# Linear attentions: the score tiles of two heads in one tile of two banks, put together by the same instructions

## The chip, the cores and the metric

The kernel runs on 1 core of one Trainium2 chip. The metric is the device time of one execution in microseconds (us). Before the change it is 2995.86 us, the median of 3 runs (2993.44 to 3003.88). Engines are named as in the profile: PE (TensorE matmuls), PEld (its weight loads), DVE (VectorE), ACT (ScalarE), POOL (GpSimd), SP (the queue that issues the DMAs).

## The reference

One layer of a hybrid encoder on 2048 tokens of width 1024. A projection `p = RMSNorm(x) @ W_in` is split among four mixers: FoX attention, a gated delta net, HGRN2 and GLA, with 4 heads each; then an output projection and a feed-forward part. The change concerns the two linear attentions, HGRN2 (key width 64) and GLA (key width 32), both of this form:

```python
def gla_chunked(q, k, v, log_a, scale):
    ...
    G = jnp.cumsum(log_a..., axis=3)
    rel = jnp.where(causal[:, :, None], G[..., :, None, :] - G[..., None, :, :], -jnp.inf)
    a_intra = jnp.einsum('bhnrd,bhnsd,bhnrsd->bhnrs', q, k, jnp.exp(rel))
    o_intra = jnp.einsum('bhnrs,bhnse->bhnre', a_intra, v)
    ...
    def step(state, inp):
        o = jnp.einsum('bhcd,bhde->bhce', qi, state)
        state = state * ai[..., None] + jnp.einsum('bhcd,bhce->bhde', ki, vi)
```

The score of a row and an earlier column is a dot product weighted by a decay that differs for every key channel, so it is no plain product of two matrices.

## The kernel before, in words

**Streams.** The tokens go in 4 blocks of 512. `phase_mix` runs four streams and weaves them by due time: `group_gdn`, `group_hg` (HGRN2), `group_gla`, and `in_proj`, which makes the projections (`proj_fm`, `proj_tm`, `mm3` at lines 107 to 110: three 128x512 matmuls for each of 8 slices) and the operands of FoX. When the projections are done, FoX (`fox_stream`) is woven with what is left of the mixers. The framework then schedules the instructions of each engine by priority; what the projections need is given priority (`first`). The order on each engine is fixed when the program is built. Rows of the order below show it.

**One linear attention.** `group_hg` and `group_gla` call `lin_attn` with `nt` = 2 and 1 (the number of 128-row tiles that the 4 heads fill). It goes through a block in 4 chunks of 128 tokens. `operands` makes, for the 7 levels h = 64, 32, ..., 1, tiles `wx` in which queries and keys carry the decay from the middle of each stretch of 2h tokens (lines 690 to 709). With these a score between the two halves of such a stretch is a plain product.

**The products.** For one group `g`, line 726 takes a tile `ps2` of one PSUM bank (128 x 512 floats; the profile calls it `ps`) from a pool of two. A group covers two head-and-chunk pairs `u`: two heads of one chunk for HGRN2, one head in two chunks for GLA; in what follows it is called a head. For each `u`, line 732 makes the 32x32 products of levels 0, 1, 2, 4, 8 and 16 for four 32-token blocks, line 736 those of level 32 and line 739 those of level 64: 56 matmuls for a head, which the profile counts as 112.

**Putting together.** Line 742 (VectorE) multiplies level 0 by a diagonal mask into `l_acc`; line 744 overlays the five other levels with masked copies, 64 columns each. Lines 751 or 753 (ScalarE, four copies) bring the four diagonal blocks to `AT`, lines 756 and 758 (two copies each) the off-diagonal blocks straight from the score tile. `AT` is one fixed tile per attention. Line 770 then multiplies it with the values, beside line 767, which adds what the state gives; line 772 takes the result off, lines 776, 778 and 782 make the state's update, line 787 applies it.

So a block holds 8 groups of HGRN2 (4 chunks x 2) and 8 of GLA (2 pairs of chunks x 4), 64 in all for 4 blocks. Both attentions share the pool `ps2`; all others (`ps`, `psl`, and `ps_mm` of the projections) are their own pools.

## Time and profile before

| what | us |
|---|---|
| median of 3 runs | 2995.86 |
| the profiled execution | 2996.68 |
| its span, first to last instruction | 2994.9 |
| TensorE matmuls busy | 2864.3 |
| VectorE busy | 2152.0 |
| ScalarE busy | 1596.3 |
| mean granted TensorE clock (share of full speed) | 0.967 |

Times in the profile are from the first instruction. Busy time of matmuls is modelled at its end, so matmuls that follow each other closely overlap in it; the starts tell their pace. A wait is listed as the engine and line that waited, and the engine and line that came last. The profile drops buffer numbers, so `ps` stands for the tiles of the pools `ps` and `ps2` alike; lines tell them apart.

### The profile page before, as it was taken

What the parts mean: (1) busy time and instruction counts of PE and PEld (TensorE: products, weight loads), DVE (VectorE), ACT (ScalarE), POOL (GpSimd) and SP (SyncE); (2) the same over time, 40 slices, a digit from 0 to 9 for tenths busy, and PEclk for the clock granted to TensorE, in tenths of its full rate; (3) what the DMA queues carried; (4) which work ended last, traced back from release to release, by engine and by line L of the source; (5) the groups of instructions that cost most, each with busy time, mean ns of one, the idle gap of its engine ahead of it and who ended that gap; (6) DMA issues with size and microseconds to landing.
All of it is one profiled execution on the core that took longest, in us unless ns stands there. A gap on an engine that the chain in (4) does not pass through costs nothing.

```text
span 2994.9 us, 57398 instructions
## 1 busy us (share of the span) xinstructions
PE 2864.3 (96%) x21994; PEld 2335.9 (78%) x21994; DVE 2152.0 (72%) x4666; ACT 1596.3 (53%) x3171; POOL 127.5 (4%) x258
## 2 busy tenths in 40 slices
PE   7999999999999998999999999999999999999999
PEld 5777777787777777777788888878788888888787
DVE  6697778678767876667666655558777777886975
ACT  6575667566656665555666632343455544544443
POOL 0000010001000100000000000003000000000000
PEclk9999999799889997999999999999999999999999
DMA  5633463355235523876533322453222221847344
GB/s 179 183 100 126 139 181 100 112 165 166 80 104 171 165 66 103 222 205 203 137 107 103 102 67 66 141 184 116 85 84 75 85 85 60 281 142 242 130 136 145
DMA packets 268938, 400.08 MB, mean 134 GB/s; under 512 B 66612, under 2 KB 93124, under 8 KB 268152
## 3 DMA queue, kind: packets, MB, share of 16 engines
q1 hardware_dynamic: 268664, 396.43, 43.5%
q8 instruction: 172, 2.82, 0.4%
q14 instruction: 102, 0.84, 0.1%
HBM read 310.63 MB, written 85.70 MB: 132 GB/s over the span
## 4 chain that ended last, share of the span: by engine, by line
PE 73%; DVE 9%; DMA 9%; ACT 6%; issue 2%; SPq 0%; DVEq 0%; ACTq 0%
PE ps_mm L108 15%; PE ps_mm L109 15%; PE ps_mm L110 14%; PE pt L108 3%; PE pt L110 3%; PE pt L109 3%; DVE w_lo L307 2%; PE po L1033 2%; DMA w_raw<-w_fm 2%; PE pt L1019 2%; PE ps L732 1%; ACT w_hi L306 1%; PE ps_mm L344 1%; PE ps_mm L346 1%; PE ps_mm L347 1%
## 5 line engine op out<-in xcount | busy, mean ns | idle before, releaser
L307 DVE TENSOR_TENSOR w_lo<-w_raw,w_hi 128x512 fp32r<-128x512 f32 x386 | 268.8, 698 | 199.7 <-ACT w_hi L306 188.1
L306 ACT CAST w_hi<-w_raw 128x512 fp32r<-128x512 f32 x386 | 237.7, 617 | 281.2 <-PE ps_mm L109 179.4
L108 PE MATMUL ps_mm<-h_hi,w_hi 128*128 128x512 f32 x736 | 314.8, 429 | 15.7 <-ACT h_hi L300 7.7
L108 PE MATMUL ps_mm<-h,w_hi 128*128 128x512 f32 x768 | 308.2, 402 | 2.6 <-ACT h L1208 1.7
L109 PE MATMUL ps_mm<-h,w_hi 128*128 128x512 f32 x768 | 303.9, 396 | 0.0
L109 PE MATMUL ps_mm<-h_lo,w_hi 128*128 128x512 f32 x736 | 303.5, 413 | 0.0
L110 PE MATMUL ps_mm<-h,w_lo 128*128 128x512 f32 x768 | 303.4, 396 | 0.0
L110 PE MATMUL ps_mm<-h_hi,w_lo 128*128 128x512 f32 x736 | 302.1, 411 | 0.5 <-issue 0.4
L108 PE MATMUL ps_mm<-big,w_hi 128*128 128x512 f32 x456 | 183.6, 404 | 11.1 <-ACT big L306 6.7
L108 PEld LDWEIGHTS ps_mm<-h_hi,w_hi 128*128 128x128 f32 x736 | 144.3, 197 | 54.8 <-ACT h_hi L300 10.5
L110 PE MATMUL ps_mm<-big,w_lo 128*128 128x512 f32 x456 | 181.8, 399 | 0.0
L109 PE MATMUL ps_mm<-big,w_hi 128*128 128x512 f32 x456 | 181.7, 399 | 0.0
L110 PEld LDWEIGHTS ps_mm<-h,w_lo 128*128 128x128 f32 x768 | 144.4, 188 | 33.8
L108 PEld LDWEIGHTS ps_mm<-h,w_hi 128*128 128x128 f32 x768 | 144.1, 188 | 33.1 <-ACT h L1208 2.7
L110 PEld LDWEIGHTS ps_mm<-h_hi,w_lo 128*128 128x128 f32 x736 | 144.6, 196 | 31.0 <-DVE w_lo L307 1.5
L109 PEld LDWEIGHTS ps_mm<-h,w_hi 128*128 128x128 f32 x768 | 144.6, 188 | 30.9 <-DVE h L1209 1.4
L109 PEld LDWEIGHTS ps_mm<-h_lo,w_hi 128*128 128x128 f32 x736 | 144.6, 196 | 30.7 <-issue 3.2
L306 ACT CAST w_hi<-fo 128x512 fp32r<-128x512 f32 x135 | 79.5, 620 | 104.4 <-issue 36.8
L1238 DVE SCALAR_TENSOR_TENSOR y<-u,fconv,y 128x512 f32<-128x512 f32 x176 | 131.8, 749 | 3.8
L1382 DVE SCALAR_TENSOR_TENSOR y<-u,fconv,y 128x1024 f32<-128x1024 f32 x88 | 112.8, 1282 | 19.5 <-ACT y L1380 18.7
L307 DVE TENSOR_TENSOR p_lo<-pt,p_hi 128x512 fp32r<-128x512 f32 (+1 forms) x144 | 93.9, 657 | 37.9 <-ACT p_hi L306 37.8
L108 PE MATMUL pt<-w_hi 128*128 128x512 f32 x308 | 120.3, 391 | 0.0
(414 smaller groups left out, 7306.4 us busy)
## 6 DMA issues: line engine op xcount, KB each, us to landing
w_raw<-w_fm SPq DMA_DIRECT2D x184, 256.0 KB, 3.1
w_raw<-w_up SPq DMA_DIRECT2D x88, 256.0 KB, 2.6
fo<-w_down SPq DMA_DIRECT2D x88, 256.0 KB, 3.5
fo<-a_scr SPq DMA_DIRECT2D x88, 256.0 KB, 4.4
wr<-w_up SPq DMA_DIRECT2D x84, 256.0 KB, 2.7
p_scr<-w SPq DMA_DIRECT2D x72, 256.0 KB, 2.7
w_raw<-w_out SPq DMA_DIRECT2D x64, 256.0 KB, 3.7
w_raw<-w_tm SPq DMA_DIRECT2D x48, 256.0 KB, 3.0
```

What stands on the lines that cost most here:

```text
L108: mm(ps, w_hi, x_hi, start=start, stop=False, **k)
L109: mm(ps, w_hi, x_lo, start=False, stop=False, **k)
L110: mm(ps, w_lo, x_hi, start=False, stop=stop, **k)
L306: self.nc.scalar.copy(out=hi, in_=src)
L307: self.nc.vector.tensor_tensor(out=lo, in0=src, in1=f32(hi), op=ALU.subtract)
L344: mm(o, self.h_hi[k][:, ts], hi[:, s], start=(k == 0 and tt % 2 == 0), stop=False, skip_group_check=True)
L346: mm(o, self.h_hi[k][:, ts], lo[:, s], start=False, stop=False, skip_group_check=True)
L347: mm(o, self.h_lo[k][:, ts], hi[:, s], start=False, stop=(k == KT - 1), skip_group_check=True)
L1019: nc.tensor.transpose(pt[:, x * 128:x * 128 + 128], P[t][:, kt * 128:kt * 128 + 128], self.ident)
L1033: mm(po[:, c0:c0 + cn], vst[:, kt], part[:, kk * 256:kk * 256 + cn], start=(kt == 0 and part is hi), stop=(kt == nkt - 1 and part is lo), ...
L1238: nc.vector.scalar_tensor_tensor(out=y, in0=u[:, i:i + TB], scalar=w(i), in1=y, op0=ALU.mult, op1=ALU.add)
L1382: nc.vector.scalar_tensor_tensor(out=yt, in0=u[g][:, i:i + 2 * TB], scalar=f(i), in1=yt, op0=ALU.mult, op1=ALU.add)
```

## The change

The pool `ps2` holds one tile of two banks in place of two tiles of one bank. Two heads are multiplied into one such tile, one into each bank; then every instruction that puts a head together works on both: 4 copies from the score tile (lines 747 and 749, now ahead of VectorE's work), the multiplication (752), five masked copies (754) and four copies from `l_acc` (758). The generator yields once for two heads, with size 2.

```diff
@@ -172,7 +172,7 @@
             self.ch = pool(ctx, "ch", 2)
             self.ps = pool(ctx, "ps", 2, space=PSUM)
             self.psl = pool(ctx, "psl", 1, space=PSUM)
-            self.ps2 = pool(ctx, "ps2", 2, space=PSUM)
+            self.ps2 = pool(ctx, "ps2", 1, space=PSUM)
             cst = self.cst_p.tile([128, N_CST], F32, name="cst")
             nc.sync.dma_start(out=cst, in_=self.i["cst"])
             self.cst = cst
@@ -723,40 +723,40 @@
             if nt == 2 or c % 2 == 0:
                 ATg = self.AT[nt - 1]
                 ATs = [ATg[:, u] for u in range(3 - nt)]
-                for g in range(per):
-                    p = self.ps2.tile([128, TB], F32, name="ps2")
+                for g0 in range(0, per, 2):
+                    p2 = self.ps2.tile([128, 2, TB], F32, name="ps2")
+                    for gg in range(2):
+                        g, p = g0 + gg, p2[:, gg]
+                        for u in range(2):
+                            h, cc = (2 * u + g, c) if nt == 2 else (g, c + u)
+                            for l, hl in enumerate((0, 1, 2, 4, 8, 16)):
+                                for blk in range(4):
+                                    mm(p[blk * 32:blk * 32 + 32, l * 64 + u * 32:l * 64 + u * 32 + 32],
+                                       at(kp if hl == 0 else Xs[hl], h, cc, blk * 32, 32),
+                                       at(qp if hl == 0 else Xs[hl], h, cc, blk * 32, 32), start=True, stop=True)
+                            for bk in (0, 64):
+                                mm(p[bk:bk + 32, 384 + u * 32:416 + u * 32], at(Xs[32], h, cc, bk, 32),
+                                   at(Xs[32], h, cc, bk + 32, 32), start=True, stop=True)
+                            for bk in (0, 32):
+                                mm(p[u * 64 + bk:u * 64 + bk + 32, 448:512], at(Xs[64], h, cc, bk, 32),
+                                   at(Xs[64], h, cc, 64, 64), start=True, stop=True)
+
+                    dst = ATs[0].rearrange("p (u g) t -> p u g t", g=2) if nt == 2 else ATg[:, :, g0:g0 + 2]
+                    ug = lambda t: t.rearrange("p g (u t) -> p u g t", u=2)
+                    for bk in (0, 64):
+                        nc.scalar.copy(out=dst[bk:bk + 32, :, :, bk + 32:bk + 64], in_=ug(p2[bk:bk + 32, :, 384:448]))
                     for u in range(2):
-                        h, cc = (2 * u + g, c) if nt == 2 else (g, c + u)
-                        for l, hl in enumerate((0, 1, 2, 4, 8, 16)):
-                            for blk in range(4):
-                                mm(p[blk * 32:blk * 32 + 32, l * 64 + u * 32:l * 64 + u * 32 + 32],
-                                   at(kp if hl == 0 else Xs[hl], h, cc, blk * 32, 32),
-                                   at(qp if hl == 0 else Xs[hl], h, cc, blk * 32, 32), start=True, stop=True)
-                        for bk in (0, 64):
-                            mm(p[bk:bk + 32, 384 + u * 32:416 + u * 32], at(Xs[32], h, cc, bk, 32),
-                               at(Xs[32], h, cc, bk + 32, 32), start=True, stop=True)
-                        for bk in (0, 32):
-                            mm(p[u * 64 + bk:u * 64 + bk + 32, 448:512], at(Xs[64], h, cc, bk, 32),
-                               at(Xs[64], h, cc, 64, 64), start=True, stop=True)
-                    acc = self.ch.tile([128, 64], F32, name="l_acc")
-                    nc.vector.tensor_tensor(out=acc, in0=p[:, 0:64], in1=self.k(K_DIAG, 64), op=ALU.mult)
+                        nc.scalar.copy(out=dst[0:64, u, :, 64:128], in_=p2[u * 64:u * 64 + 64, :, 448:512])
+                    two = lambda t: t.rearrange("p (g t) -> p g t", g=2)
+                    acc = self.ch.tile([128, 2, 64], F32, name="l_acc")
+                    nc.vector.tensor_tensor(out=acc, in0=p2[:, :, 0:64], in1=two(self.k(K_DIAG, 128)), op=ALU.mult)
                     for l in range(5):
-                        nc.vector.copy_predicated(out=acc, mask=self.lvmask[:, l, 0:64],
-                                                  data=p[:, (l + 1) * 64:(l + 2) * 64])
-                    u2 = lambda t: t.rearrange("p (u t) -> p u t", u=2)
-                    AT = ATs[0].rearrange("p (u g) t -> p u g t", g=2)[:, :, g] if nt == 2 else None
+                        nc.vector.copy_predicated(out=acc, mask=two(self.lvmask[:, l]),
+                                                  data=p2[:, :, (l + 1) * 64:(l + 2) * 64])
                     for blk in range(4):
                         s = slice(blk * 32, blk * 32 + 32)
-                        if nt == 2:
-                            nc.scalar.copy(out=AT[s, :, s], in_=u2(acc[s]))
-                        else:
-                            nc.scalar.copy(out=ATg[s, :, g, s], in_=u2(acc[s]))
-                    dst = AT if nt == 2 else ATg[:, :, g]
-                    for bk in (0, 64):
-                        nc.scalar.copy(out=dst[bk:bk + 32, :, bk + 32:bk + 64], in_=u2(p[bk:bk + 32, 384:448]))
-                    for u in range(2):
-                        nc.scalar.copy(out=dst[0:64, u, 64:128], in_=p[u * 64:u * 64 + 64, 448:512])
-                    yield
+                        nc.scalar.copy(out=dst[s, :, :, s], in_=ug(acc[s]))
+                    yield 2
             more = c < 3 and (c + 1) * 128 % span == 0
             if more:
                 ahead = operands((c + 1) * 128)
```

The order changes at these places. On TensorE, in the second block: the end of one head of GLA (`ps_5809`; its score tile, with the number of this build), and the next head, of HGRN2 (`ps_5934`). Before:

```order
L739 MATMUL ps_5809<-wx 32x64 x2
L732 MATMUL ps_5934<-wl 32x32 x4
L732 MATMUL ps_5934<-wx 32x32 x20
L736 MATMUL ps_5934<-wx 32x32 x2
L739 MATMUL ps_5934<-wx 32x64 x2
L732 MATMUL ps_5934<-wl 32x32 x4
L732 MATMUL ps_5934<-wx 32x32 x20
L736 MATMUL ps_5934<-wx 32x32 x2
L739 MATMUL ps_5934<-wx 32x64 x2
L770 MATMUL psl<-wl,AT_153 128x64
L110 MATMUL ps_mm<-h_hi_3383,w_lo 128x512
```

After, the end of the third tile of that block (`ps_5852`, two heads of GLA) and the first rows behind it:

```order
L741 MATMUL ps_5852<-wx 32x64 x2
L770 MATMUL psl<-wl,AT_153 128x64 x4
L110 MATMUL ps_mm<-h_hi_3361,w_lo 128x512
L108 MATMUL ps_mm<-h_hi_3368,w_hi 128x512
L109 MATMUL ps_mm<-h_lo_3369,w_hi 128x512
```

Five rows later comes the fourth tile (`ps_6448`, two heads of HGRN2), behind these:

```order
L782 MATMUL psl<-wl,l_kT 128x128 x2
L108 MATMUL ps_mm<-h_hi_3382,w_hi 128x512
L109 MATMUL ps_mm<-h_lo_3383,w_hi 128x512
L110 MATMUL ps_mm<-h_hi_3382,w_lo 128x512
L108 MATMUL ps_mm<-h_hi_3333,w_hi 128x512
L734 MATMUL ps_6448<-wl 32x32 x4
L734 MATMUL ps_6448<-wx 32x32 x20
```

Before, the second head's products stand right behind the first's; after, 11 projection matmuls (`L108` to `L110`) and eight small ones (`L770`, `L776` and `L782`) stand between two tiles.

On VectorE, one head of the same stretch before (`ps_5934`):

```order
L742 TENSOR_TENSOR l_acc<-ps_5934,cst 128x64
L581 TENSOR_REDUCE X_5717<-x16t 128x11
L744 COPY_PREDICATED l_acc<-lvmask,ps_5934 128x64
L579 TENSOR_TENSOR x16t<-X_5717,D_5707 128x144
L744 COPY_PREDICATED l_acc<-lvmask,ps_5934 128x64
L581 TENSOR_REDUCE X_5717<-x16t 128x12
L744 COPY_PREDICATED l_acc<-lvmask,ps_5934 128x64
L307 TENSOR_TENSOR w_lo<-w_raw,w_hi 128x512
L120 TENSOR_SCALAR w_6441<-w_6441 128x512
L744 COPY_PREDICATED l_acc<-lvmask,ps_5934 128x64
L579 TENSOR_TENSOR x16t<-X_5717,D_5707 128x169
L744 COPY_PREDICATED l_acc<-lvmask,ps_5934 128x64
```

And the two heads of `ps_5852` after:

```order
L752 TENSOR_TENSOR l_acc<-ps_5852,cst 128x128
L695 TENSOR_TENSOR wx<-wl 128x128
L754 COPY_PREDICATED l_acc<-lvmask,ps_5852 128x128
L697 TENSOR_TENSOR wx<-wx,wl 128x64x2
L754 COPY_PREDICATED l_acc<-lvmask,ps_5852 128x128
L698 TENSOR_TENSOR wx<-wx,wl 128x64x2
L754 COPY_PREDICATED l_acc<-lvmask,ps_5852 128x128
L697 TENSOR_TENSOR wx<-wx,wl 128x128
L754 COPY_PREDICATED l_acc<-lvmask,ps_5852 128x128
L698 TENSOR_TENSOR wx<-wx,wl 128x128
L754 COPY_PREDICATED l_acc<-lvmask,ps_5852 128x128
```

The six operations of a head are now the six of two heads, twice as wide, still with other work between them.

On ScalarE, before: the eight copies of the head `ps_5934` (`AT_153` is the fixed tile of HGRN2, `AT_152` that of GLA):

```order
L121 ACTIVATE w_6441<-w_6441 128x512
L122 ACTIVATE w_6441<-w_6441 128x512
L751 COPY AT_153<-l_acc 32x2x32 x2
L114 ACTIVATE w_6349<-ps_mm,eps 128x512
L751 COPY AT_153<-l_acc 32x2x32
L115 ACTIVATE w_6349<-w_6349 128x512
L751 COPY AT_153<-l_acc 32x2x32
L756 COPY AT_153<-ps_5934 32x2x32 x2
L758 COPY AT_153<-ps_5934 64x64 x2
```

After: the four copies from `ps_5852`, and later the four from its `l_acc`:

```order
L882 ACTIVATE w_6174<-w_6172,cols 128x512
L747 COPY AT_152<-ps_5852 32x2x2x32 x2
L749 COPY AT_152<-ps_5852 64x2x64 x2
L772 COPY wl<-psl 128x2x128
L696 ACTIVATE wx<-wx 128x256 x2
L778 COPY l_kT<-psl 128x256
L306 CAST w_hi<-w_raw 128x512
L872 COPY w_6442<-ps_mm 128x512
L758 COPY AT_152<-l_acc 32x2x2x32
L873 ACTIVATE w_6445<-w_6442 128x512
L758 COPY AT_152<-l_acc 32x2x2x32 x3
```

The copies from the score tile stood last and now stand first; what follows the masked copies is four copies from `l_acc` for two heads.

## Rows read from the trace of the kernel before

**Rows 1.** The page: span; busy us, share and instructions by engine.

```profile
span 2994.9 us, 57398 instructions
...
PE 2864.3 (96%) x21994; PEld 2335.9 (78%) x21994; DVE 2152.0 (72%) x4666; ACT 1596.3 (53%) x3171; POOL 127.5 (4%) x258
```

**Rows 2.** Busy time by stretch; columns: us, busy (instructions) by engine, PEclk, DMA share, GB/s.

```profile
400.00:500.00 100.00, 93.44 (x1228) 72.88 (x1227) 86.51 (x285) 69.98 (x168) 8.67 (x7) 0.95 0.44 132
1010.00:1040.00 30.00, 27.87 (x225) 21.34 (x224) 29.39 (x83) 19.94 (x42) 7.28 (x2) 0.94 0.46 138
1120.00:1140.00 20.00, 18.68 (x431) 15.58 (x429) 12.54 (x49) 9.57 (x33) 0.00 (x0) 0.74 0.40 113
```

**Rows 3.** Tile `l_acc`: ns min/median/max, first and last start us, shapes.

```profile
L744 DVE COPY_PREDICATED l_acc<-lvmask,ps x320: 202/222/235, 183.9 to 1189.8; 128x64 f32<-128x64 uint8 x160
L753 ACT COPY AT<-l_acc x128: 238/242/249, 186.3 to 1161.9; 32x64 f32<-32x64 f32 x128
L751 ACT COPY AT<-l_acc x128: 227/241/246, 188.2 to 1190.9; 32x64 f32<-32x64 f32 x128
L742 DVE TENSOR_TENSOR l_acc<-ps,cst x64: 207/218/227, 183.5 to 1184.2; 128x64 f32<-128x64 f32 x64
```

**Rows 4.** Tile `AT` (same columns); then who waited for `L758` (us, times).

```profile
L756 ACT COPY AT<-ps x128: 185/203/208, 187.3 to 1191.4; 32x64 f32<-32x64 f32 x128
L758 ACT COPY AT<-ps x128: 193/208/210, 187.7 to 1191.9; 64x64 f32<-64x64 f32 x128
...
  PEld psl L770: 12.5, 10
  PEld ps L732: 11.8, 15
  PE psl L770: 8.5, 8
  PE ps L732: 6.3, 11
```

**Rows 5.** Groups by line and shape, 140 to 1240 us: count, busy us, mean ns, idle before.

```profile
L697 DVE TENSOR_TENSOR wx<-wx,wl 128x128 f32<-128x128 f32 x168 | 47.9, 285 | 22.1 <-ACT wx L696 21.7
...
L657 ACT COPY g_vn<-ps 64x256 f32<-64x256 f32 x32 | 11.7, 367 | 30.5 <-PE ps L654 30.3
```

**Rows 6.** TensorE in order of time: start, us, instruction, [idle before <-releaser].

```profile
471.25 0.26 PE L732 MATMUL ps<-wl 32*32 32x32 f32 x8 [0.45 <-ACT AT L758]
...
473.15 0.27 PE L732 MATMUL ps<-wl 64*32 64x32 f32 x8 [0.55 <-ACT AT L758]
...
474.23 0.28 PE L739 MATMUL ps<-wx 64*32 64x64 f32 x3
...
475.46 0.63 PE L108 MATMUL ps_mm<-h_hi,w_hi 128*128 128x512 f32 x1
475.88 0.63 PE L109 MATMUL ps_mm<-h_lo,w_hi 128*128 128x512 f32 x1
...
479.05 0.26 PE L732 MATMUL ps<-wl 32*32 32x32 f32 x8
...
480.66 0.40 PE L109 MATMUL ps_mm<-h_lo,w_hi 128*128 128x512 f32 x1
480.89 0.39 PE L110 MATMUL ps_mm<-h_hi,w_lo 128*128 128x512 f32 x1
...
483.17 0.88 PE L770 MATMUL psl<-wl,AT 128*128 128x64 f32 x6 [0.97 <-ACT AT L758]
```

**Rows 7.** VectorE and ScalarE in order of time, the same head.

```profile
475.86 0.21 DVE L742 TENSOR_TENSOR l_acc<-ps,cst 128x64 f32<-128x64 f32 x1
...
479.01 0.22 DVE L744 COPY_PREDICATED l_acc<-lvmask,ps 128x64 f32<-128x64 uint8 x1
...
482.91 0.44 ACT L758 COPY AT<-ps 64x64 f32<-64x64 f32 x2
```

**Rows 8.** Busy time by stretch, columns as in rows 2.

```profile
474.40:477.80 3.40, 3.40 (x13) 2.46 (x9) 2.83 (x19) 1.73 (x6) 0.00 (x0) 0.51 0.02 5
480.40:483.80 3.40, 2.43 (x13) 1.79 (x13) 2.65 (x9) 3.21 (x10) 0.00 (x0) 1.00 0.22 80
```

## The prediction

> **What bounds the kernel now.** I read the page's totals first, then busy time by stretch, then the answers on the tiles `AT` and `l_acc`, then one hand-over in order of time. The totals show TensorE busy for 2864.3 of 2994.9 us and VectorE for 2152.0 [rows 1]: the kernel is bound by TensorE, so an instruction taken from VectorE or ScalarE gains only where TensorE waits for it. The stretches show where that can be: in 400 to 500 us TensorE is busy for 93.4 of 100 us; in 1010 to 1040 us, where operands, the small inverse and the score assembly of one block meet, VectorE is busy for 29.4 of 30; in 1120 to 1140 us, when the projections are done, VectorE and ScalarE have 12.5 and 9.6 of 20 and the granted clock is 0.74 [rows 2]. The touched code runs from 184 to 1190 us [rows 3], in four blocks; the code behind it is unchanged. The profiled execution took 2996.68 us, 0.8 above the median of the three runs; the sum is made against it.
>
> **VectorE and ScalarE instructions.** Before, each of the 64 heads-and-chunks groups takes one multiplication and five masked copies on VectorE (64 x 0.218 + 320 x 0.222 = 85 us) and eight copies on ScalarE (256 x 0.242 from `l_acc`, 128 x 0.203 and 128 x 0.208 from the score tile = 115 us) [rows 3, 4]. After, there are half as many, each twice as wide. No row shows a masked copy of 128 columns. Its bounds are the 0.222 of 64 columns and twice that; I take 0.285, the row of a 128x128 VectorE product [rows 5]. That gives 192 x 0.285 = 55 us, so VectorE is rid of 30 us (0 to 42 by the bounds). For ScalarE the rows 64x64 at 0.208 and 64x256 at 0.367 [rows 4, 5] give 0.053 us for 64 further columns: 128 x 0.295 + 128 x 0.26 = 71 us, so ScalarE is rid of 44 us. Nearly all of it lies beside TensorE's work and counts for nothing by itself.
>
> **TensorE.** Products, their order inside a head and their count stay; this costs nothing.
>
> **Waits that end earlier (-16.2 us).** TensorE's weight loads wait 12.5 us (`L770`, for the last piece of `AT`) and 11.8 us (`L732`, for the score buffer) behind the last of the eight ScalarE copies, 24.3 us together; of its matmuls the same waits hold 14.8 us [rows 4]. In the order of time one such case stands: a head's first product waits 0.55 us at 473.15, its last product ends at 474.51, its last masked copy on VectorE starts at 479.01 and ends at 479.23, and its last ScalarE copy ends only at 483.35, which then lets `L770` go after 0.97 us of idle [rows 6, 7]. After the change the four copies that read the score tile go ahead of VectorE's work, and behind the last masked copy there remain four copies of 0.295 (1.2 us) for two heads, in place of two times eight with 1.8 us each (4 x 0.242 + 2 x 0.203 + 2 x 0.208). So 1.2/3.6 of the wait is left and two thirds of 24.3 us go: -16.2. The bounds are 0, if other ScalarE work moves into the gap, and -24.3.
>
> The Trainium skill, in "Perfetto Trace Analysis", section "Optimizing Scalar/DVE Operations", says that where ScalarE and VectorE aren't saturated but cause bubbles on others, *breaking up* instructions lets work finish sooner; this change does the opposite. By that rule this term would be 0 and the sum 2996.7 - 5 + 6 + 4 = 3002 instead of 2985, the upper end of the rival *no change* below. The trace of before has only the narrow instructions and cannot show it.
>
> **The tail (-5 us).** In the last block four pairs run with no projections to cover them. A saving of 3.6 - 1.2 = 2.4 us on each pair's chain would be 9.6 us at most; the other end is 0, as `L770` waits only on a few of them. I take the middle.
>
> **New waits for the single score tile (+6 us).** Before, a second buffer lets the next head's products follow without a gap. After, the first product of a pair waits until the last masked copy of the pair before has read both banks. Two hand-overs of a block are close in the order: between its second and third pair stand 18 projection matmuls and one of two passes, between its third and fourth 11 with eight small ones; ahead of the other six stands more. (In the last block the projections end early, and the tail above is what covers its last pairs.) A projection matmul starts 0.23 us behind the one before at full clock [rows 6], so that is 18 x 0.23 + 0.46 = 4.6 us of cover at the first, and at the second 2.5 us with some 1.7 for the small ones (two passes each, six passes of `L770` in 0.88 us [rows 6]), 4.2 us. Against it stands the time from the last product to the last masked copy: 4.7 us for the head above [rows 6, 7]. For a pair, the six operations are wider by 6 x 0.063 = 0.4 us, so 5.1 us. The shortfall is 0.5 to 0.9 us at two hand-overs in each of four blocks: 8 x 0.75 = +6. The lower end is 0. The upper end is the 8.8 us in which that head is wholly put away (474.51 to 483.35): (8.8 - 4.4) x 8 = +35.
>
> **The clock (+4 us).** Behind the two heads' products that ran back to back from 471.25 to 474.51 the granted clock is 0.51, that is the 1.2 GHz level, from 474.4 to 477.8; behind the single head that starts at 479.05 it is 1.00, from 480.4 on [rows 6, 8]. At the low level projection matmuls start 0.42 us apart (475.46, 475.88) against 0.23 [rows 6], so such a stretch of 3.4 us costs 3.4 x (1 - 0.23/0.42) = 1.5 us. After the change each pair is such a double burst. But a mean of 0.95 in 400 to 500 us [rows 2] is 10 of the 100 us at the low level, three such stretches already, and this part of a block will hold four pairs; at most two further ones a block are 4 x 2 x 1.5 = +12. The lower end is 0, or below if fewer bursts let the clock up. I take +4.
>
> **Sum.** -16.2 - 5 + 6 + 4 = -11.2: 2996.7 - 11.2 = 2985.5, in round numbers **2985 us**, or 0.36% below the median.
>
> **Rivals.** *The single tile decides (slower).* The masked copies of a pair stand between other VectorE work, on which the queue waits in order, and the release comes as late as the 8.8 us above. Then the hand-overs cost 35 instead of 6: 2985.5 + 29 = 3014 us. It decides against the change once the last masked copy ends over 4.4 + (16.2 + 5 - 4)/8 = 6.6 us behind the pair's products on average. For it: in 1010 to 1040 us VectorE has no slack [rows 2], and the six operations of the head above, 1.3 us by themselves, are spread from 475.86 to 479.23 by other work [rows 7]. Against it: half the instructions, and only two close hand-overs a block. The Trainium skill speaks for it: "Perfetto Trace Analysis", section "Matmuls", wants independent groups to rotate through banks so that putting away one overlaps the next. Here the rotation ends; the trace has only rotating buffers.
>
> *The clock decides (slower).* If every pair drops the clock and the drops last twice as long, 4 x 8 x 1.5 = 48 in place of 4: 3029 us at worst, 3007 at half of that. For it: the double burst at 471. Against it: 0.95 over a window that already holds the products of eight heads.
>
> *No change.* The waits behind ScalarE move to another late instruction (an operand `wx`, a projection's weights) since the whole stage is TensorE work: the -16.2 falls away and the hand-overs cost 0 to 6: 2996.7 - 5 + 4 = 2996 to 3002 us, the lower end likelier. For it: TensorE is busy for 93% there [rows 2]. Against it: the waits are named for `L758`, at 25 weight loads.
>
> *More than forecast.* If all of the 24.3 us go, the tail gives 10 and the hand-overs and the clock cost nothing: 2962 us.
>
> That the change does not do what it says can be left out: the order shows the halved rows.
>
> **Chances.** Forecast 0.36 and more than forecast 0.06; no change 0.30; the single tile 0.19; the clock 0.09. A measurement of this kernel tells about 0.3% (9 us) from no change. Faster by more: 0.36 + 0.06 = 0.42; within: 0.30; slower by more: 0.19 + 0.09 = 0.28. The range of 8 in 10 goes from 2966 to 3014; the forecast's own range is 2972 to 2992.
>
> **What the next profile would show.** Right: masked copies x160 at about 0.285, copies x256, VectorE's total down by some 30 us and ScalarE's by 44, the waits for the last copy into `AT` below 8 us, the mean clock within 0.005 of 0.967, the mixers done some 10 us sooner. Wrong: first products (`L734`) waiting for the last masked copy (`L754`) for over 20 us in all, or a mean clock of 0.96 or less, or VectorE down by 30 us with the same end, which would mean that the copies had been cover for nothing.

## The result, and the profile after

The changed kernel takes 3015.11 us (median of 12 runs, 3005.71 to 3024.11) against 2995.63 us before (12 runs on the same chips): a ratio of 1.0062, with a 95% interval of 1.0041 to 1.0083. It is slower by some 19 us, 0.6%, clear of the interval, and 1 us above the upper end of the range. The profiled execution took 3020.37 us, 23.7 us more than that of before (2996.68).

The page's totals of the changed kernel, beside [rows 1]:

```profile
span 3018.6 us, 56953 instructions
...
PE 2862.6 (95%) x21994; PEld 2351.7 (78%) x21994; DVE 2141.3 (71%) x4474; ACT 1555.3 (52%) x2915; POOL 126.5 (4%) x258
```

ScalarE is rid of 41.0 us and VectorE of 10.7; TensorE is busy for as long as before, in a longer span. The tiles `l_acc` and `AT` of the changed kernel, columns as in [rows 3], then who waited for `L754` and, last, for `L749` (us, times):

```profile
L754 DVE COPY_PREDICATED l_acc<-lvmask,ps x160: 282/297/308, 184.8 to 1205.3; 128x128 f32<-128x128 uint8 x160
L758 ACT COPY AT<-l_acc x128: 279/295/300, 188.9 to 1206.6; 32x128 f32<-32x128 f32 x128
L752 DVE TENSOR_TENSOR l_acc<-ps,cst x32: 283/292/294, 184.2 to 1198.9; 128x128 f32<-128x128 f32 x32
...
  PE ps L734: 3.2, 3
  PEld ps L734: 0.4, 1
```

```profile
L747 ACT COPY AT<-ps x64: 237/256/258, 175.1 to 1198.0; 32x128 f32<-32x128 f32 x64
L749 ACT COPY AT<-ps x64: 248/261/263, 175.9 to 1198.6; 64x128 f32<-64x128 f32 x64
...
  DVE l_acc L752: 36.3, 18
```

The instructions are what they were priced at. TensorE no longer waits for the last copy into `AT` (24.3 us of weight loads before [rows 4], nothing now), and for the single score tile its products wait 3.2 us in all, in three places. So the waits on which the prediction rests came out well. What TensorE's weight loads wait for from 140 to 1240 us (engine, tile, line, what it waited for: us, times, longest), in the changed kernel and then in the kernel before:

```profile
PEld ps L734 <- issue: 49.8, 40, 3.6
```

```profile
PEld ps L732 <- issue: 18.8, 43, 2.2
```

"Issue" is a wait for nothing that the profile shows, and at the products it grew by 31 us in about as many places. In order of time one such place, a pair's products on TensorE:

```profile
588.86 0.27 PE L734 MATMUL ps<-wx 32*32 32x32 f32 x7
591.38 0.42 PE L734 MATMUL ps<-wx 32*32 32x32 f32 x28 [2.25 <-issue]
...
591.72 0.27 PE L741 MATMUL ps<-wx 32*32 32x64 f32 x3
```

TensorE stops for 2.25 us **in the middle of a row of products**. No instruction there has a semaphore to wait for, and the tile is the pair's own already. In the trace's list of transfers, a load of instructions of 16,384 bytes starts at 588.45 and takes 1.31 us. Of stops over 0.8 us inside a row (60 or more matmuls and weight loads behind its first), the changed kernel has 16 with 38.9 us, the kernel before 3 with 5.5. In 15 of the 16 such a load is in flight during the stop. At a row's first product the waits with no cause did not grow (9.3 us, before 13.0): all of the growth is inside rows (41.4 us, before 5.9). The second thing that moved is the clock. Busy time by stretch, as in [rows 2], of the changed kernel and then of the kernel before:

```profile
140.00:1240.00 1100.00, 1011.92 (x13312) 839.40 (x13310) 797.38 (x2199) 616.70 (x1378) 36.21 (x24) 0.90 0.42 127
```

```profile
140.00:1240.00 1100.00, 1033.21 (x13423) 841.08 (x13421) 822.54 (x2437) 669.90 (x1666) 39.38 (x24) 0.92 0.44 131
```

By the trace's record of the granted clock, TensorE ran at the 1.2 GHz level for 218.4 us of the first 1300, against 177.5 before; after that the two are alike (21.7 and 20.5 us). The last product ends at 1197.7 us, before at 1177.2, and the last matmul behind `AT` (`L770`) at 1214.8, before at 1192.8: 22.0 of the 23.7 us are lost by then.

### The profile page after: what moved, and what is told of

Its sections match the earlier page's. It is cut to its first block, busy times and chain, and to the rows that moved or that the text cites. A ratio compares the mean times of both kernels' runs of the same rounds, so it can differ in the third digit from the quotient of the medians.

```text
span 3018.6 us, 56953 instructions
## 1 busy us (share of the span) xinstructions
PE 2862.6 (95%) x21994; PEld 2351.7 (78%) x21994; DVE 2141.3 (71%) x4474; ACT 1555.3 (52%) x2915; POOL 126.5 (4%) x258
## 4 chain that ended last, share of the span: by engine, by line
PE 77%; DMA 9%; DVE 7%; ACT 3%; issue 3%; SPq 1%; DVEq 0%; ACTq 0%
PE ps_mm L108 15%; PE ps_mm L109 15%; PE ps_mm L110 15%; PE pt L108 3%; PE pt L110 3%; PE pt L109 3%; DVE w_lo L307 2%; PE ps L734 2%; PE po L1033 2%; PE pt L1019 2%; PE ps_mm L344 1%; PE ps_mm L346 1%; PE ps_mm L347 1%; PE psl L770 1%; PE ps L607 1%
## 5 line engine op out<-in xcount | busy, mean ns | idle before, releaser
L306 ACT CAST w_hi<-w_raw 128x512 fp32r<-128x512 f32 x386 | 237.3, 617 | 287.5 <-PE ps_mm L109 194.6
L108 PE MATMUL ps_mm<-h_hi,w_hi 128*128 128x512 f32 x736 | 318.6, 435 | 16.6 <-ACT h_hi L300 7.8
L108 PE MATMUL ps_mm<-h,w_hi 128*128 128x512 f32 x768 | 308.6, 403 | 3.4 <-ACT h L1208 2.5
L110 PE MATMUL ps_mm<-h_hi,w_lo 128*128 128x512 f32 x736 | 307.8, 418 | 0.1
L110 PE MATMUL ps_mm<-h,w_lo 128*128 128x512 f32 x768 | 303.5, 396 | 0.0
L108 PEld LDWEIGHTS ps_mm<-h_hi,w_hi 128*128 128x128 f32 x736 | 148.1, 202 | 56.8 <-ACT h_hi L300 10.6
L108 PE MATMUL ps_mm<-big,w_hi 128*128 128x512 f32 x456 | 182.7, 401 | 7.3 <-ACT w_hi L306 3.5
L110 PE MATMUL ps_mm<-big,w_lo 128*128 128x512 f32 x456 | 180.2, 396 | 0.0
L110 PEld LDWEIGHTS ps_mm<-h_hi,w_lo 128*128 128x128 f32 x736 | 147.9, 201 | 33.8 <-DVE w_lo L307 1.5
L108 PEld LDWEIGHTS ps_mm<-h,w_hi 128*128 128x128 f32 x768 | 144.3, 188 | 34.0 <-ACT h L1208 3.8
L110 PEld LDWEIGHTS ps_mm<-h,w_lo 128*128 128x128 f32 x768 | 144.5, 188 | 33.6
L109 PEld LDWEIGHTS ps_mm<-h,w_hi 128*128 128x128 f32 x768 | 144.7, 188 | 30.6 <-DVE h L1209 0.9
L108 PE MATMUL pt<-w_hi 128*128 128x512 f32 x308 | 120.4, 391 | 0.0
```

Source lines behind the costliest of these rows:

```text
L108: mm(ps, w_hi, x_hi, start=start, stop=False, **k)
L109: mm(ps, w_hi, x_lo, start=False, stop=False, **k)
L110: mm(ps, w_lo, x_hi, start=False, stop=stop, **k)
L306: self.nc.scalar.copy(out=hi, in_=src)
```

## The experiments

Three theories were set against each other, named in the texts on record: **A**, unbroken rows of 112 products run TensorE out of instructions; **B**, the single score tile decides; **C**, rows of small products pull the clock down. "Row" is a run of products with nothing else between in TensorE's order. Ratios are to the kernel before, in the same comparison, with 95% intervals.

### One part undone at a time

**e1: a pause between the two heads.**

```diff
                 for g0 in range(0, per, 2):
+                    while self.p2_held:
+                        yield 0.02
+                    self.p2_held = True
...
                     for gg in range(2):
+                        if gg:
+                            yield 1
...
-                    yield 2
+                    self.p2_held = False
+                    yield 1
```

The flag keeps the other linear attention from starting a pair of its own in the pause.

> The changed kernel with one thing undone: between the products of the pair's first head and those of its second there is a pause in which other work may be queued, so that TensorE no longer gets 112 decay products in an unbroken row at most places; the two-bank tile, the wide masked copies and the wide ScalarE copies all stay, and so does the order of everything else but for the place of the pauses (one unit after each head, where the change has two after the pair). Theory A (unbroken rows of 112 small products run TensorE out of instructions in mid-row): the idle time at the products that ends with no wait (89 us over the program in the changed kernel, 25 us before) falls to 20 to 45 us, and the time is 2985 to 3002 us, a ratio of 0.996 to 1.002 to the kernel before. Theory B (one score tile where there were two: TensorE, or the work queued behind the next products, waits for the tile): the tile is held longer here than in the changed kernel, so the time is 3015 us or more, ratio 1.006 or more. Theory C (the clock falls because long rows of small products look like rest to it): the mean clock comes back from 0.960 to 0.965 or more and the time to 2990 to 3002 us even if the idle time stays.

Measured: 3026.99 us, 1.0106 (1.0071 to 1.0140). Rows of 112 or 108 fell only from 22 to 8: at the first pair of each of the two attentions in every block, the two heads' products still follow each other unbroken. 9 stops of 20.8 us were left. The waits with no cause fell from 50.7 to 39.7 us, as A wanted, and the time did not follow; it lies in B's range (3015 or more). What rose is the time at the low clock: the mean granted clock of these six executions is 0.957, that of the kernel before in the same comparison 0.966, which makes some 260 us at the low level against 200. So C's return of the clock did not come either. Against A alone.

**e2: one tile instead of two, nothing else.**

```diff
-            self.ps2 = pool(ctx, "ps2", 2, space=PSUM)
+            self.ps2 = pool(ctx, "ps2", 1, space=PSUM)
```

> The kernel before with one of its two score tiles taken away, and nothing else: products, narrow instructions and order of one head at a time stay. Theory A (long rows starve TensorE): no row is longer than before, so 2994 to 3005 us, ratio 0.999 to 1.003, and the idle time at the products that ends with no wait stays near 25 us. Theory B (the single tile decides): 3010 us or more, ratio 1.005 or more, with TensorE's products waiting for the last masked copy or the last ScalarE copy from the tile for 20 us or more. Theory C (the clock): as before, 0.965 or more, unless the waits for the tile pull it down.

Measured: 3027.07 us, 1.0103 (1.0071 to 1.0134), with no stop in a row at all. TensorE's weight loads in this kernel, 140 to 1240 us:

```profile
PEld ps L732 <- ACT AT L758: 27.0, 25, 2.0
PEld psl L770 <- ACT AT L758: 15.4, 16, 1.5
PEld ps L732 <- issue: 7.0, 22, 0.7
```

The waits for the last copy rose from 24.3 to 42.4 us, those with no cause fell from 18.8 to 7.0. B is right about the tile: with narrow instructions, giving up the second one costs 34 us, and A's range is missed. The clock fell too (262.8 us at the low level).

**e3: the two-bank tile and its long rows, but narrow instructions,** head by head as before.

```diff
-                    acc = self.ch.tile([128, 2, 64], F32, name="l_acc")
...
+                    for gg in range(2):
+                        g, p = g0 + gg, p2[:, gg]
+                        acc = self.ch.tile([128, 64], F32, name="l_acc")
...
```

> The changed kernel's two-bank tile and its products of both heads in one row, but put together as before, with one multiplication, five masked copies and eight ScalarE copies per head. Theory A (long rows starve TensorE): the rows of 112 are there, so the idle time at the products that ends with no wait stays well above 25 us (40 to 90) and the time is 3005 to 3025 us, ratio 1.003 to 1.010; the wide instructions are not what costs. Theory B (the single tile decides): the tile is held longer than in the changed kernel, since twelve short instructions stand where six wide ones stood, so the time is above 3025 us, ratio above 1.010. Rival D (the wide instructions themselves cost: a pair's masked copies come later than a single head's would): 2990 to 3002 us, ratio at most 1.002.

Measured: 3076.01 us, 1.0260 (1.0233 to 1.0288): above A's range, in B's open one (above 3025), and D falls. Waits for copies (28.4 us) and stops (13 with 26.1 us) come together here. It is 61 us above the changed kernel, but not by the narrow instructions alone, since the copies from the score tile stand last here, as before; beside e4, which has wide instructions and the same place of the copies, they cost 23 us.

**e4: the copies from the score tile last, as before.**

```diff
-                    for bk in (0, 64):
-                        nc.scalar.copy(out=dst[bk:bk + 32, :, :, bk + 32:bk + 64], in_=ug(p2[bk:bk + 32, :, 384:448]))
-                    for u in range(2):
-                        nc.scalar.copy(out=dst[0:64, u, :, 64:128], in_=p2[u * 64:u * 64 + 64, :, 448:512])
...
                         nc.scalar.copy(out=dst[s, :, :, s], in_=ug(acc[s]))
+                    for bk in (0, 64):
...
```

> The changed kernel with only ScalarE's order changed: the four copies straight from the score tile come behind the four from the put-together tile, as before, and not ahead of the multiplication. VectorE's multiplication waits 36 us in 18 places for those copies in the changed kernel. Theory A (long rows starve TensorE): that wait goes or shrinks, the idle time at the products stays (70 to 100 us with no wait), and the time stays at 3008 to 3020 us, ratio 1.004 to 1.008. Theory B (the single tile decides): the last reader of the tile is now a ScalarE copy that comes after all masked copies, so the tile comes free at another time and the time moves by over 5 us against the changed kernel. Rival E (the wait of the multiplication is what the change lost): 2990 to 3003 us, ratio at most 1.002.

Measured: 3052.52 us, 1.0195 (1.0161 to 1.0229). 37 us above the changed kernel: A's range is missed, E falls, and the moment at which the tile comes free does matter. The stops stayed (19 with 39.5 us).

**e5: two tiles of one bank, narrow instructions, long rows.**

```diff
+                for g0 in range(0, per, 2):
+                    ps = []
+                    for g in (g0, g0 + 1):
+                        p = self.ps2.tile([128, TB], F32, name="ps2")
...
+                        ps.append(p)
+                    for g in (g0, g0 + 1):
+                        p = ps[g - g0]
...
+                    yield 2
```

> The kernel before with its two tiles of one bank and its narrow instructions, but with the products of two heads in one row and only then the two heads put together, so that rows of 112 products come often (14 of them, 3 before). It differs from the narrow variant of the two-bank tile only in that each head's bank comes free by itself. Theory A (long rows starve TensorE in mid-row): pauses in mid-row of 25 us or more in sum (5.5 us before) and 3005 to 3025 us, ratio 1.004 to 1.010. Theory B (what decides is when the next products find a free tile): the first bank of the pair comes free half a pair earlier than a two-bank tile would, so the time is near the kernel before and far below the narrow two-bank variant (ratio 1.026): 2995 to 3010 us, ratio 1.000 to 1.005, whatever the pauses in mid-row.

Measured: 3010.06 us, 1.0056 (1.0031 to 1.0081): in A's range and just outside B's, with 18.4 us of stops in rows, fewer than A said. Long rows cost some 16 us even where both tiles are kept and their readers are waited for no longer than before (21.2 us, before 24.3).

**e6: the kernel before, copies from the score tile first.**

```diff
+                    for bk in (0, 64):
+                        nc.scalar.copy(out=dst[bk:bk + 32, :, bk + 32:bk + 64], in_=u2(p[bk:bk + 32, 384:448]))
+                    for u in range(2):
+                        nc.scalar.copy(out=dst[0:64, u, 64:128], in_=p[u * 64:u * 64 + 64, 448:512])
                     acc = self.ch.tile([128, 64], F32, name="l_acc")
...
```

> The kernel before with only ScalarE's order changed, the other way round from the variant of the change with its copies last: the four copies straight from the score tile come first, ahead of the multiplication, and the four from the put-together tile last. Theory B (what decides is when the tile comes free): the score tile comes free with the last masked copy, not with the last of eight ScalarE copies, so TensorE's waits for the last copy go down from 24 us to under 12 us and the time falls to 2975 to 2990 us, ratio 0.993 to 0.998. Theory A (long rows): no row is longer, so no change, ratio 0.998 to 1.002. A rival: VectorE's multiplication now waits for the copies as in the changed kernel, about 1 us for each head, and the time is 2998 us or more.

Measured: 2994.06 us, 0.9991 (0.9971 to 1.0010). The waits for the last copy went from 24.3 to 5.0 us, as B wanted, but the waits with no cause at the products rose from 19.8 to 38.6 us, and nothing was gained: the time lies in A's range, though for another reason than A gave. Of the rise, 11.7 us are stops inside rows (17.6 us, before 5.9), although no row is longer, and 5.9 stand at the first products of rows. This was the first sign that the two can take each other's place, as if **a TensorE that waits for a tile were supplied with instructions meanwhile**; no run tests that by itself.

**e7: each head's row cut in two, with a pause.**

```diff
                 for g in range(per):
+                    while self.p2_held:
+                        yield 0.02
+                    self.p2_held = True
...
                     for u in range(2):
+                        if u:
+                            yield 0.5
...
-                    yield
+                    self.p2_held = False
+                    yield 0.5
```

The flag is that of e1.

> The kernel before with each head's products cut in two rows of 28 with half a unit's pause between them, in which other work may be queued; tiles and instructions as before. Theory C (rows of small products pull the clock down): the time at half clock below 1300 us falls from 177 us to under 150 us, and the time to 2975 to 2990 us, ratio 0.993 to 0.998. Theory B (when the tile comes free decides): the tile is held longer, so the time is 2998 us or more, ratio above 1.001. Theory A (long rows): the pauses in mid-row (5.5 us before) go, which by itself is a gain of up to 6 us.

Measured: 3025.54 us, 1.0091 (1.0061 to 1.0121), 194.6 us at the low level. C's gain did not come: rows of half a head did not hold the clock up. The waits for the tile's readers rose from 24.3 to 32.1 us, as B wanted.

**e11: one tile, narrow, copies first,** that is the edits of e2 and e6 together.

> The kernel before with one score tile and the four copies straight from it first: one head at a time, narrow instructions, rows of one head. Beside the variant with one tile and the copies last (ratio 1.010) it prices the copies, beside the changed kernel (ratio 1.006) the merging of two heads. Theory B (when the single tile comes free decides): the tile comes free with the last masked copy, and so the time is 3003 to 3018 us, ratio 1.003 to 1.008, at least 8 us below the variant with the copies last. Theory A (long rows): no pauses in mid-row beyond those of the kernel before with its copies first (15 us), and 2990 to 3002 us, ratio at most 1.003.

Measured: 3023.07 us, 1.0087 (1.0054 to 1.0120). Hardly better than e2, within the intervals, so B's range (to 3018) was missed, and A's (to 3002) by more. The weight loads' wait for the tile fell from 27.0 to 0.4 us and their waits with no cause rose from 8.8 to 37.9, but not as in e6: no row has a stop inside, and nearly all of it stands at a row's first product. There the matmul behind the weight load waits for the last masked copy (140 to 1240 us):

```profile
PE ps L732 <- DVE l_acc L751: 13.4, 10, 3.8
```

These ten places hold 15.6 of the 37.9 us. It is still a wait for the single tile, as B has it, now ended by VectorE and not by ScalarE; the other places are short, 0.37 us each.

### The supply of instructions, by itself

**e8: one head's products four times over** in each GLA block of the kernel before, into the same tile, so that the repeats wait for nothing.

```diff
+                    for _ in range(4 if nt == 1 and g == 0 else 1):
                     for u in range(2):
```

> The kernel before with the products of one head of each GLA block issued four times over into the same tile (8 rows of 224 products, 448 of TensorE's instructions for each operand pass and as many weight loads, waiting for nothing after the first). Only where the pauses come is looked at, not the time. Theory A (TensorE runs out of instructions): each such row stops at least two or three times for 1 to 3 us, at about equal distances in instructions, with a load of instructions of 16 KB at about the time of each stop. Its rival (the pauses in mid-row are hidden waits for data or for the tile): such rows show no more pauses than the rows of before, since the repeated products wait for nothing.

The first such row of the second block, in order of time, and the same stretch cut at its stops (columns as in [rows 2]: us, TensorE's matmuls, its weight loads, ..., granted clock):

```profile
475.55 0.26 PE L737 MATMUL ps<-wx 32*32 32x32 f32 x1 [2.10 <-issue]
...
479.00 0.69 PE L733 MATMUL ps<-wx 32*32 32x32 f32 x35 [1.17 <-issue]
```

```profile
471.18:473.44 2.26, 2.26 (x211) 2.15 (x211) 2.26 (x10) 0.63 (x3) 0.00 (x0) 0.98 0.50 155
473.44:475.54 2.10, 0.00 (x1) 0.00 (x0) 2.10 (x12) 1.30 (x4) 0.00 (x0) 0.50 0.26 91
475.54:477.83 2.29, 2.28 (x128) 2.15 (x128) 2.29 (x12) 1.17 (x4) 0.00 (x0) 0.50 0.03 7
477.83:479.00 1.17, 0.00 (x1) 0.00 (x1) 1.17 (x6) 0.75 (x2) 0.00 (x0) 0.50 0.00 0
479.00:481.50 2.50, 2.50 (x103) 2.23 (x104) 1.69 (x10) 0.00 (x0) 0.00 (x0) 0.50 0.03 7
```

A row here is 440 or 448 matmuls and as many weight loads. Between the two stops stand exactly 128 matmuls and 128 weight loads, 256 instructions, and in all eight such rows the second stop, and the third where there is one, comes 256 instructions after the one before. The first stop of a row takes 2.0 to 3.4 us, the later ones 1.1 to 2.3. Instruction loads of 16,384 bytes start at 472.93, 476.72 and 480.13 us and take 1.0 to 1.4 us each: 16,384 / 256 is 64 bytes an instruction. The queue of these loads is TensorE's: it makes 193 of them for the 49,364 matmuls and weight loads of this kernel, and 172 for the 43,988 of the kernel before, one for every 256. This is shown: a row of small products eats a load (256 instructions in 2.3 us) faster than the next arrives (3.4 to 3.8 us apart), and then TensorE stands. The granted clock goes to 0.50, the 1.2 GHz level, at 473.34, after 2.2 us of these products and 0.1 us ahead of the first stop, and stays there for the rest of the row.

The Trainium skill has the block in "Runtime: NRT & Kernel Launch", section "Instruction fetch mechanics": instructions are refilled in blocks of 16 KiB, 256 instructions. The trace agrees to the instruction. The same section calls the cost of crossing a block mostly hidden; here it shows for 1.1 to 3.4 us, so for rows of small products the measurement decides.

### The change without the long rows

**e9 and e10: both kernels with four of the six levels of products left out,** all masked copies kept.

```diff
-                            for l, hl in enumerate((0, 1, 2, 4, 8, 16)):
+                            for l, hl in enumerate((0, 16)):
...
-                                                  data=p2[:, :, (l + 1) * 64:(l + 2) * 64])
+                                                  data=p2[:, :, 64:128])
```

> The kernel before with four of each head's six levels of products left out (distances 1, 2, 4 and 8); the masked copies are all there and read the level of distance 16 each, so that the tile is held as long as before. It stands only beside the changed kernel with the same levels left out. Both theories: faster than the kernel before, since 2048 of 3584 small products (each about 24 ns in two passes) are gone: 2930 to 2965 us, ratio 0.978 to 0.990, with hardly a pause in mid-row.

> The changed kernel with the same four levels of products left out and all masked copies kept, each reading the level of distance 16. A pair's row is now 48 products, shorter than one head's row in the full kernel, while the one two-bank tile, the wide instructions and the order stay. Theory A (the pauses in mid-row are what the change lost): the pauses go, and it is as fast as the thinned kernel before or faster, by up to 15 us. Theory B (the single tile is what it lost): it stays slower than the thinned kernel before by 12 to 25 us, with no pauses in mid-row.

Measured: 2967.01 us (0.9907, 0.9873 to 0.9942; 2 us above its range) and 2907.03 us (0.9707, 0.9674 to 0.9740). With a pair's row of 48 products, the merged kernel is **60 us faster** than its counterpart, on one tile. Neither has a stop in a row. TensorE's weight loads at the products and at `L770`, in the thinned kernel before and then in the thinned change:

```profile
PEld ps L732 <- issue: 17.1, 36, 3.3
PEld ps L732 <- ACT AT L758: 15.3, 18, 1.4
PEld psl L770 <- ACT AT L758: 14.5, 17, 2.4
```

```profile
PEld ps L734 <- issue: 12.2, 21, 2.9
```

A's direction, beyond its 15 us; B falls for the merged kernel. But a thinned pair is also less work for TensorE, so instructions and work are not yet apart. The tile is held no shorter: from a pair's first product to the end of its last masked copy it is 16.4 us on average, in the changed kernel 15.4.

**e12 and e13: the same levels replaced by products of four times the columns,** in both kernels: nearly as much TensorE time, little over half of the instructions, and all readers of the tile kept.

```diff
+                            for blk, hl in enumerate((1, 2, 4, 8)):
+                                mm(p[blk * 32:blk * 32 + 32, 64 + u * 128:192 + u * 128],
+                                   at(Xs[hl], h, cc, blk * 32, 32), at(Xs[hl], h, cc, 0, 128), start=True, stop=True)
-                            for l, hl in enumerate((0, 1, 2, 4, 8, 16)):
+                            for l, hl in ((0, 0), (5, 16)):
```

> The kernel before with four of each head's six levels of products (distances 1, 2, 4 and 8: 32 products of 32 columns for a head) replaced by 8 products of 128 columns each, whose results mean nothing; all other products, the masked copies and the ScalarE copies are there. TensorE has nearly the same work for a head (1.35 us for 112 short products of a pass, 12 ns each; four times the columns for a quarter of the instructions), but about half as many instructions. It stands beside the changed kernel with the same replacement. Both theories: within 2 per cent of the kernel before, 2960 to 3010 us, with no pauses in mid-row.

> The changed kernel with the same replacement: a pair's row is 64 products instead of 112, about as long in time as before but with little over half of the instructions; the tile is held as long as in the changed kernel, by all of its readers. Theory A (the number of instructions in a row, that is the supply of them, is what the change lost): the pauses in mid-row (38.9 us in the changed kernel) fall below 12 us and it is faster than its own kernel before, by 20 to 65 us. Theory B2 (the thinned kernels gained because each pair's work and the hold of its tile became shorter): it is as slow beside its kernel before as the change was, between 10 us faster and 25 us slower, with or without pauses.

Measured: 2997.35 us (1.0009, 0.9988 to 1.0029) and 2967.58 us (0.9909, 0.9877 to 0.9942): merged, it is **30 us faster**, one stop in a row is left (2.0 us), and the waits for copies are gone (30.6 us in e12, 0.4 in e13). From product to product inside rows TensorE spends 74.0 us in e13, or 72 without its stop, against 82 in the changed kernel without its stops (120.8 - 38.9); in e12 it is 74.2, so what is missing is missing on both sides. The last masked copy ends 8.4 us behind a pair's last product, in the changed kernel 7.8. A is right, B2 falls: the number of instructions in a row turns a gain of 30 us into a loss of 19.

**e14: the second head's products strewn among other work.** They get a slightly lower rank in the order.

```diff
+                        with self.tc.high_priority(offset=-10 if gg else 0):
                         for u in range(2):
```

> The changed kernel with one thing changed: the second head's products have a slightly lower rank in the order than what is written behind them, so that they are strewn among the other products (mean row 61 products, weighted by length, 91 in the changed kernel and 54 in the kernel before), without a pause asked for between the heads. Theory A (rows): the pauses in mid-row fall from 39 to under 20 us, and the time to 2970 to 2998 us, ratio 0.992 to 1.001. Theory B2 (how long the tile is held): a pair's products take half as long again to issue as in the changed kernel (estimated from the order, 7 against 4.5 us in the mean), so the time is 3012 us or more, ratio 1.006 or more.

Measured: 3160.61 us, 1.0551 (1.0526 to 1.0576): the worst of all, and for a reason that neither theory had. The stops inside rows fell to 8 with 19.8 us, just as A said, but TensorE's order now has 406 rows of products instead of 63, and entering them costs:

```profile
PEld ps L735 <- issue: 83.3, 212, 2.8
```

Nine of the 212 waits, 21.4 us, stand inside rows; the other 203 come at a row's first product, 0.31 us each. Not all of that is lost: behind a 128x512 matmul the first product starts after 0.43 us where the next 128x512 would after 0.23 (medians at full clock). The time lies in B2's open range (3012 or more), but the readers of the tile are waited for by 0.7 us only, so not by its mechanism. Cutting rows finely is no way out, and no version of the full computation was found that beats both kernels.

### All runs in one table

Standing still is the sum of TensorE's weight-load waits from 140 to 1240 us at the products and behind `AT`: for a tile's readers, and at the products with no cause shown. The time at the low level is that before 1300 us. A matmul step of 0.42 us at that level against 0.23 [rows 6] makes each such microsecond cost 1 - 0.23/0.42 = 0.45 us. "Worked" is the difference in standing still plus 0.45 times that in low time, to the kernel before (for e10 to e9 and for e13 to e12, whose own values stand in brackets); "measured" the same difference of the profiled spans.

| kernel | wait for copies, tile | no cause | low clock | worked | measured | median us |
|---|---|---|---|---|---|---|
| before | 24.3 | 19.8 | 177.5 | | | 2994 |
| change | 0.4 | 50.7 | 218.4 | +25 | +23.7 | 3015 |
| e1 pause | 4.5 | 39.7 | 211.6 | +15 | +19.7 | 3027 |
| e2 one tile | 42.4 | 8.8 | 262.8 | +45 | +41.3 | 3027 |
| e3 narrow | 28.4 | 38.2 | 300.4 | +78 | +80.6 | 3076 |
| e4 copies last | 13.6 | 53.7 | 266.2 | +63 | +50.3 | 3053 |
| e5 two tiles, rows | 21.2 | 31.2 | 177.5 | +8 | +9.6 | 3010 |
| e6 copies first | 5.0 | 38.6 | 211.6 | +15 | -5.3 | 2994 |
| e7 half heads | 32.1 | 28.3 | 194.6 | +24 | +28.9 | 3026 |
| e11 one tile, first | 12.2 | 37.9 | 252.6 | +40 | +33.3 | 3023 |
| e14 strewn | 0.7 | 97.6 | 316.4 | +117 | +163.1 | 3161 |
| e10 (e9) | 2.5 (29.8) | 12.7 (19.7) | 116.0 (235.5) | -88 | -77.2 | 2907 (2967) |
| e13 (e12) | 0.4 (30.6) | 13.6 (9.4) | 187.7 (201.4) | -32 | -36.9 | 2968 (2997) |

Standing still and the low clock account for most rows within 13 us; e6 is off by 20, and why is open. e14 is off by 46 only because its products run on to 1343 us, past the stretch: over the whole program it stands still for 112.5 us (before 44.1) and is at the low level for 401.5 (before 198.0), which makes 68 + 92 = 160 against 163. In e11, part of "no cause" is a wait for the tile, as said there.

The table has one execution of each kernel, and the clock differs between executions of the same kernel. Over the 64 executions of the kernel before on record, 0.001 less of mean granted clock goes with 2.3 us more (a fitted line), or 0.38 us for each microsecond at the low level, near the 0.45 above. e1's median lies 11 us above its profiled execution because the others ran at a lower clock, on average.

## Why the prediction was wrong, point by point

**Instructions: right.** Masked copies 0.297 us (0.285 forecast), copies 0.295 and 0.26 (as forecast). ScalarE's total fell by 41 us. VectorE's fell by 10.7, not 30: masked copies and multiplications fell by 28.3 us, and other VectorE instructions (`wx`, `w_lo`) took longer; why was not tried.

**Waits that end earlier (-16.2): right in kind, too small.** 24.3 us became 0.4, the far bound. (In the case that the prediction shows, `L770` starts at 483.17, ahead of the end of the last copy at 483.35: it waited for the copy before.) The rule of the Trainium skill on *breaking up* instructions ("Perfetto Trace Analysis", "Optimizing Scalar/DVE Operations"), which would have made this term 0, did not hold here: the waits went with instructions twice as wide, and e3, which puts the same tile away in pieces, takes 23 us more than e4 with its copies in the same place.

**The tail (-5): did not come.** Three pairs are multiplied there, not four. From the start of the last projection matmul to the end of the last `L770` it takes 69.2 us, before 69.3. The 22 us were lost ahead of it.

**New waits for the single tile (+6): right in size.** 3.2 us of matmul waits, 0.4 of weight loads. The last masked copy ended 7.8 us behind a pair's products on average, over the 6.6 us from which the rival was to decide, yet the products waited for only 3.2 us, so that point was set too low.

**"Products, their order inside a head and their count stay; this costs nothing": the step that failed.** Order and count inside a head do stay; the row does not. Two heads together are 448 of TensorE's instructions without a pause, where one load is 256. This term, put at nothing, measured some +31 us: waits with no cause at the products rose by 30.9 us, those inside rows by 35.5. The trace of before held the sign: 18.8 us of "issue" at `L732`, of which 5.5 us in three stops, at the few places where heads ran back to back. e8 shows the mechanism, e13 its price for the change.

**The clock (+4, at most +12): mis-sized.** 40.9 us more at the low level are 18 us. The +4 stood for some three further stretches of 3.4 us; these are twelve. That is the one profiled execution of each kernel. By the mean granted clock, 0.9618 in the 12 executions of the changed kernel and 0.9654 in the 64 of the kernel before, it is some 23 us more at the low level, or 10 us.

With measured sizes the sum is -23.9 + 30.9 + 18.4 = +25 us, and the spans differ by 23.7. Of the rivals, *the single tile decides* gave the nearest time (3014), but by luck: e2 shows that its mechanism exists (34 us with narrow instructions, as the Trainium skill's "Perfetto Trace Analysis", "Matmuls", would have it), e10 and e13 that it is not what the wide instructions suffer from. *The clock decides* names 18 of the 49 us that were lost in the profiled execution, but the clock did not go with the length of a row: e2, with no row longer than a head's, is lower than the change.

What stays open: what moves the clock (e1 waits as long as the kernel before and is lower; e5 waits 8 us longer and is not), why e6 does not follow the two columns, and why a load comes too late at some places and not at others.

## What to carry to other kernels

Count TensorE's instructions in an unbroken row, weight loads included, before joining small matmuls: from about one load of 256 on, a row can pay a stop of 1 to 3.5 us that no semaphore shows, and "issue" in mid-row with an instruction load beside it is its mark (16 stops in the changed kernel with its rows of 448; one in e13, whose longest rows are 256). A wait that is taken away can uncover such a stop (e6, where the stops inside rows rose as the waits fell): price both together. And look behind "issue" at a row's first weight load for what its matmul waits for (e11). The change as a whole was worth 30 us where the rows stay short in instructions, by fewer and wider products (e13 beside e12).

## What the runs showed of the hardware that was not expected

- TensorE stops every 256 instructions in a row of small products, for 1.1 to 3.4 us, and loads 16,384 bytes of instructions at each stop (e8); its loads are one for every 256 instructions in all kernels here.
- Behind a 128x512 matmul the first small product of a row starts later than the next 128x512 matmul would: after 0.43 us (e14, 172 places) or 0.33 us (the kernel before, 55 places) where that one does after 0.23 (medians at full clock). "TensorEngine Tiling (Array Packing)", section "Key Properties", of the Trainium skill says that a change of the tiling mode drains TensorE. No run isolates that as the reason; if it is, this is its first price in these runs.
- Four products of 128 columns in place of sixteen of 32 left the kernel before as fast as it was (1.0009), with 3072 of TensorE's 21994 matmuls fewer.
